# Moving half of the probability scaling to GpSimd and half of the transposed copies to VectorE in a sparse-attention decoder kernel

## The chip, the cores and the metric

The kernel runs on one core of a Trainium2 chip. The metric is the device time in microseconds (us) of one execution, as the median of several runs. The engines are called PE (TensorE), PEld (its weight loads), DVE (VectorE), ACT (ScalarE), POOL (GpSimd) and SP (SyncE, which issues DMAs).

## What is computed

The reference is a two-layer decoder trunk on 256 tokens of width 1024, in float32. Layer 0 mixes tokens with a gated MLP, layer 1 with a sparse attention of three branches (compressed, selected blocks, window); each layer ends in a squared-ReLU MLP of width 4096. With 256 tokens the selected-block branch selects all blocks and the window covers all tokens, so both are causal softmax attention, with two different K/V sets. There are 16 query heads in 4 groups of 4 heads, head size 64. What the change touches is this part:

```python
s_sel = jnp.einsum('bqghd,bgqmd->bghqm', qb, ks)
p_sel = masked_softmax(s_sel, kpos <= tq[None, None, None, :, None])
o_sel = jnp.einsum('bghqm,bgqmd->bqghd', p_sel.astype(vs.dtype), vs)
...
p_w = masked_softmax(s_w, mask_w)
o_win = jnp.einsum('bghqk,bkgd->bqghd', p_w.astype(vw.dtype), vw)
o = gb[..., 0:1] * ocb + gb[..., 1:2] * o_sel + gb[..., 2:3] * o_win
```

## The kernel before

The tokens are two chunks of 128 (ck 0 and 1). Each chunk is a Python generator that goes through gMLP, MLP, attention and MLP; `drive` (L968) takes steps of the two in turn, so that one chunk's matmuls lie beside the other's vector work. A scheduler then orders each engine's instructions once, when the program is built, by priority and by durations that it models; on the chip every engine runs its list in that order, and a waiting instruction holds up all behind it. Weights are split into a high and a low part as they arrive, by one ACT copy (L350) and one DVE subtraction (L351) of 128x1024 each, and every product is three matmuls (L375 to L377). SP issues the weight loads; POOL does memsets, the small reciprocal roots (L402, L411, L412, L619) and a few DMA issues.

In the attention, `queries` (L778) makes the transposed queries of two head groups, a pair p2. `scores` (L820) makes one group's scores of both branches on PE (L835, L837), their negated maxima on DVE (L838) and the exponentials on ACT with their sums (L842), in tiles `p` of 128 x 2 branches x 128 (ck 0) or 256 keys (ck 1). `weighted` (L848) is called once per chunk and pair, four times in all, with both groups of the pair (gg 0 and 1):

- Factors `cf` (L856, L857, DVE): gate over sum, one tiny tile per group.
- Scaling (L863, DVE): each head's row of probabilities times its factor, in place, SBUF to SBUF. Per branch four heads of gg 0, then four of gg 1: 16 instructions in a call, 64 in all.
- Per branch and block kc of 128 keys (one block for ck 0, two for ck 1): for each group four transposes on PE (L871) into one PSUM tile `ptp` of 128x512 (the pool has two buffers), and a copy `pT` to SBUF on ACT (L873); 24 copies in all.
- Products with the values (L876), gg 0 in columns 0 to 63 of the array and gg 1 in 64 to 127. The line `together(m, pTs[1][1])` (L879) makes the first group's product wait for the second group's copy, so that they run side by side.

`attend_cmp` (L881) then adds the compressed branch: a chain of small DVE operations `sm`, `cden`, `pc` (L892 to L906), two transposes (L909), an ACT copy (L912) and products (L915). The chunk's output projection y_mix follows in `nsa_out` (L948).

Of the kernel before, what the change touches and what calls it, by code (L numbers as in the profile page):

```python
# [10 lines left out]
AF = mybir.ActivationFunctionType  # L11
ALU = mybir.AluOpType
# [38 lines left out]
def trunk(ctx: ExitStack, tc: tile.TileContext, x, vec, rowv, first_w, ada_w, ada_b, norm_g, a_w_in, a_w_s, a_w_out,  # L51
          kv_w, cmp_w1, cmp_b1, cmp_w2, cmp_b2, b_w_in, gate_w, b_w_out, ff_w_in, ff_w_out, out):
    nc = tc.nc
# [16 lines left out]
    def pt_tile(name, dt=F32):  # L70
        return psT.tile([P, 512], dt, tag="t", name=name)
# [63 lines left out]
    def together(ins, last):  # L135
        tc.add_manual_dep(ins.ins, last.ins.name,
                          mybir.DependencyInfo(mybir.DependencyClass.Sync, mybir.DependencyReason.DATA),
                          reason="column tiles side by side")
# [253 lines left out]
    def small(name, n=1):  # L392
        return sp.tile([P, 16], F32, tag="small", name=name)[:, :n]
# [454 lines left out]
    def weighted(ck, p2, made, oT):  # L848

        V = at["V"]  # L850
        gate = at["gate"][ck]
        cfs = []
        for gg, (pr, den) in enumerate(made):
            g = 2 * p2 + gg
            cf = small(f"cf_{ck}_{g}", 8)
            nc.vector.reciprocal(cf, den)  # L856
            nc.vector.tensor_tensor(cf.rearrange("p (h r) -> p h r", r=2), cf.rearrange("p (h r) -> p h r", r=2),  # L857
                                    gate[:, 4 * g:4 * g + 4, 1:3], ALU.mult)
            cfs.append(cf)
        for br in range(2):  # L860
            for (pr, den), cf in zip(made, cfs):
                for h in range(4):
                    nc.vector.tensor_scalar(pr[h][:, br, :], pr[h][:, br, :], cf[:, h * 2 + br:h * 2 + br + 1],  # L863
                                            None, ALU.mult)
            for kc in range(ck + 1):
                pTs = []
                for gg, (pr, den) in enumerate(made):
                    g = 2 * p2 + gg
                    pt = pt_tile(f"ptp_{ck}_{g}_{br}_{kc}")
                    for h in range(4):  # L870
                        nc.tensor.transpose(pt[:, h * P:(h + 1) * P], pr[h][:, br, kc * P:(kc + 1) * P], ident)  # L871
                    pT = rp.tile([P, 512], F32, tag="rh", name=f"pT_{ck}_{g}_{br}_{kc}", bufs=4)
                    pTs.append((pT, nc.scalar.activation(pT, pt, AF.Copy)))  # L873
                for gg in range(2):
                    g = 2 * p2 + gg
                    m = nc.tensor.matmul(oT[64 * gg:64 * gg + 64, :], V[:, kc, br, g * 64:g * 64 + 64], pTs[gg][0],  # L876
                                         start=(br == 0 and kc == 0), stop=False)
                    if gg == 0:
                        together(m, pTs[1][1])  # L879
# [38 lines left out]
    def nsa(ck, parts):  # L918
        nm = f"mix1_{ck}"
        xT = tmp(f"xT_{nm}")  # L920
        for hf in range(2):
            nc.scalar.activation(xT[:, half(hf)], parts[hf], AF.Copy)
        kvpair = modulated(f"kv_{ck}", parts, "kvsh", "kvsc")
        yield from keys_values(ck, kvpair)
        pool = state["np"]
        bpair = modulated(f"b_{ck}", [xT[:, half(0)], xT[:, half(1)]], "sh11", "sc11")
        yield from gates(ck, bpair)
        hh = hl = None
        for p2 in range(2):
            yield from queries(ck, bpair, p2, pool)  # L930
            oT = y_tile(f"oT_{ck}_{p2}")
            made = []
            for gg in range(2):
                made.append((yield from scores(ck, 2 * p2 + gg, pool)))
            weighted(ck, p2, made, oT)
            if ck == 0:
                yield lambda: "cmp" in at
            attend_cmp(ck, p2, oT)
            if p2 == 0:
                o0 = oT  # L940
            else:
                hh, hl = hpair(f"o_{ck}")
                for i, o in enumerate((o0, oT)):
                    split_out(hh[:, 4 * i:4 * i + 4, :], hl[:, 4 * i:4 * i + 4, :], blocks(o))
            yield
        at[f"o{ck}"] = (hh, hl)
# [166 lines left out]
```

## Time and profile before

| | |
|---|---|
| median of 3 runs | 712.33 us (711.68 to 713.01) |
| the profiled execution, its own time | 708.8 us |
| its span in the profile | 707.1 us |
| busy: PE, DVE, ACT, POOL | 666.4, 475.2, 355.9, 37.0 us |
| instructions | 9173 |
| stage of the four `weighted` calls | 421.9 to 496 us |

A row of a group of instructions names its line, engine, operation, written tile <- read tiles, shapes and count; then busy time and mean duration in ns of one; then the idle time of the engine before them and what ended it. Busy time counts overlapping instructions once, so that count times mean can be more. A row of the timeline gives start and length in us of one instruction or of a run of like instructions, and in brackets idle time before it. A row of busy time by stretch gives the stretch, its length, the busy time (and instructions) of PE, PEld, DVE, ACT and POOL, the granted clock of TensorE as a share of 2.4 GHz, the share of the DMA engines, and GB/s.

### The profile page before, as it was taken

Reading aid. Unit: us, or ns where it says so; the run is one execution under the profiler, and the core shown is the slowest. Engines: PE = TensorE matmul, PEld = TensorE weight load, DVE = VectorE, ACT = ScalarE, POOL = GpSimd, SP = SyncE. Lnnn points to the kernel's source line nnn. Section 1 sums busy time; section 2 is a strip of 40 time slices with the busy share of each in tenths; the row PEclk is TensorE's granted clock in tenths of the full one; section 3 lists DMA queues with packets and bytes.
Section 4 is the critical chain, followed back from the end, with each engine's and each line's share of the span. In section 5 each row is a group of like instructions: output and inputs, shape, how many; then the busy total and the mean of one; then the engine's idle time right before and its main releaser. Section 6 shows DMA issues by size and latency. Waiting matters only on the chain.

```text
span 707.1 us, 9173 instructions
## 1 busy us (share of the span) xinstructions
PE 666.4 (94%) x3296; PEld 499.6 (71%) x3296; DVE 475.2 (67%) x712; ACT 355.9 (50%) x599; POOL 37.0 (5%) x70
## 2 busy tenths in 40 slices
PE   4899998999999999998899989989999999999996
PEld 1456765778888888876557666656778888888884
DVE  3546984998497886959875366665887545455524
ACT  3334345665535553454535476764656555455521
POOL 3001100100000000002000000000210000000000
PEclk9999999999999999999899999999999999999999
DMA  8887879779688979855675783200576656665101
GB/s 344 343 331 287 303 298 359 238 246 374 216 291 312 390 248 363 305 211 196 193 256 201 299 327 118 90 32 1 186 252 224 210 201 209 213 209 200 63 0 60
DMA packets 45535, 162.61 MB, mean 230 GB/s; under 512 B 5417, under 2 KB 5801, under 8 KB 45490
## 3 DMA queue, kind: packets, MB, share of 16 engines
q1 hardware_dynamic: 44928, 161.82, 64.1%
q8 instruction: 26, 0.43, 0.3%
q10 hardware_dynamic: 466, 0.20, 0.1%
q14 instruction: 19, 0.16, 0.1%
q0 software_dynamic: 96, 0.01, 0.0%
HBM read 160.96 MB, written 1.05 MB: 229 GB/s over the span
## 4 chain that ended last, share of the span: by engine, by line
PE 82%; DVE 5%; ACT 5%; DMA 3%; issue 2%; POOL 2%; SPq 0%; ACTq 0%; DVEq 0%; POOLq 0%
PE y_ff L377 8%; PE y_ff L375 8%; PE y_ff L376 8%; PE pa_fi L375 8%; PE pa_fi L377 8%; PE pa_fi L376 8%; PE pts_ff L488 2%; PE ptp L871 2%; PE pa_ain L376 2%; PE pa_ain L375 2%; PE oT L876 2%; PE pa_ain L377 2%; PE y_mix L375 2%; PE y_mix L376 2%; PE pa_kv L375 2%
## 5 line engine op out<-in xcount | busy, mean ns | idle before, releaser
L351 DVE TENSOR_TENSOR wl_fo<-w_fo,wh_fo 128x1024 fp32r<-128x1024 f32 x64 | 78.1, 1224 | 53.5 <-ACT wh_fo L350 53.3
L376 PE MATMUL y_ff<-wl_fo,rh_ff 128*128 128x512 f32 x256 | 103.0, 402 | 0.0
L375 PE MATMUL pa_fi<-wh_fi,hh_ff 128*128 128x512 f32 x256 | 100.3, 392 | 2.8 <-ACT hh_ff L380 2.8
L350 ACT ACTIVATE wh_fo<-w_fo 128x1024 fp32r<-128x1024 f32 x64 | 67.5, 1059 | 68.0 <-PE pa_fi L377 52.7
L375 PE MATMUL y_ff<-wh_fo,rh_ff 128*128 128x512 f32 x256 | 101.7, 397 | 0.0
L377 PE MATMUL y_ff<-wh_fo,rl_ff 128*128 128x512 f32 x256 | 101.3, 396 | 0.0
L376 PE MATMUL pa_fi<-wl_fi,hh_ff 128*128 128x512 f32 x256 | 99.9, 390 | 0.0
L377 PE MATMUL pa_fi<-wh_fi,hl_ff 128*128 128x512 f32 x256 | 99.6, 390 | 0.0
L351 DVE TENSOR_TENSOR wl_fi<-w_fi,wh_fi 128x1024 fp32r<-128x1024 f32 x64 | 77.5, 1224 | 28.4 <-ACT wh_fi L350 27.9
L350 ACT ACTIVATE wh_fi<-w_fi 128x1024 fp32r<-128x1024 f32 x64 | 67.1, 1058 | 52.2 <-PE y_ff L377 49.4
L375 PEld LDWEIGHTS pa_fi<-wh_fi,hh_ff 128*128 128x128 f32 x256 | 48.1, 188 | 13.5 <-ACT hh_ff L380 3.7
L375 PEld LDWEIGHTS y_ff<-wh_fo,rh_ff 128*128 128x128 f32 x256 | 48.2, 188 | 10.8
L377 PEld LDWEIGHTS y_ff<-wh_fo,rl_ff 128*128 128x128 f32 x256 | 48.3, 189 | 10.2
L376 PEld LDWEIGHTS y_ff<-wl_fo,rh_ff 128*128 128x128 f32 x256 | 48.4, 189 | 9.9
L377 PEld LDWEIGHTS pa_fi<-wh_fi,hl_ff 128*128 128x128 f32 x256 | 48.1, 188 | 10.1
L376 PEld LDWEIGHTS pa_fi<-wl_fi,hh_ff 128*128 128x128 f32 x256 | 48.1, 188 | 9.9
L502 ACT ACTIVATE r_ff<-pa_fi 128x512 f32<-128x512 f32 x32 | 19.1, 595 | 36.1 <-PE pa_fi L377 36.1
L195 DVE SCALAR_TENSOR_TENSOR acc_g<-aw_g,cact,acc_g 128x1024 f32<-128x1024 f32 x24 | 30.8, 1283 | 6.7 <-DMA aw_g<-in_ada_w_dram 4.1
L842 ACT ACTIVATE p<-sc,mx 128x128 f32<-128x128 f32 (+1 forms) x64 | 26.1, 428 | 11.2 <-DVE mx L838 11.2
L375 PE MATMUL pa_ain<-wh_ain,hh_mix 128*128 128x512 f32 x64 | 26.3, 422 | 2.5 <-ACT hh_mix L380 2.1
L838 DVE TENSOR_REDUCE mx<-sc 128x2 f32<-128x512 f32 (+1 forms) x24 | 16.0, 687 | 18.8 <-PE sc L837 18.8
L381 DVE TENSOR_TENSOR rl_ff<-pts_ff,rh_ff 128x512 fp32r<-128x512 f32 x32 | 21.9, 686 | 7.8 <-ACT rh_ff L380 7.7
(291 smaller groups left out, 1169.4 us busy)
## 6 DMA issues: line engine op xcount, KB each, us to landing
w_fi<-in_ff_w_in_dram SPq DMA_DIRECT2D x64, 512.0 KB, 4.6
w_fo<-in_ff_w_out_dram SPq DMA_DIRECT2D x64, 512.0 KB, 4.5
aw_g<-in_ada_w_dram SPq DMA_DIRECT2D x32, 512.0 KB, 4.2
aw_sh<-in_ada_w_dram SPq DMA_DIRECT2D x24, 512.0 KB, 5.0
aw_sc<-in_ada_w_dram SPq DMA_DIRECT2D x24, 512.0 KB, 5.8
aw_first<-in_first_w_dram SPq DMA_DIRECT2D x16, 512.0 KB, 6.8
w_ain<-in_a_w_in_dram SPq DMA_DIRECT2D x16, 512.0 KB, 6.7
w_kv<-in_kv_w_dram SPq DMA_DIRECT2D x12, 512.0 KB, 4.3
```

Source lines behind the costliest of these rows:

```text
L195: nc.vector.scalar_tensor_tensor(acc, raw, cs, acc, ALU.mult, ALU.add)
L350: i1 = nc.scalar.activation(hi[:, :n], raw[:, :n], AF.Copy)
L351: i2 = nc.vector.tensor_tensor(lo[:, :n], raw[:, :n], hi[:, :n].bitcast(F32), ALU.subtract)
L375: nc.tensor.matmul(ps, hh, wh, start=start, stop=False)
L376: nc.tensor.matmul(ps, hh, wl, start=False, stop=False)
L377: nc.tensor.matmul(ps, hl, wh, start=False, stop=stop)
L381: nc.vector.tensor_tensor(lo, src, hi.bitcast(F32), ALU.subtract))
L488: nc.tensor.transpose(pt[:, j * P:(j + 1) * P], src[:, j * P:(j + 1) * P], ident)
L502: nc.scalar.activation(r, pa, AF.Relu)
L838: nc.vector.tensor_reduce(mx.rearrange("p (i r) -> p i r", r=2), sc, AX.X, ALU.max, negate=True)
L842: nc.scalar.activation(pr[h0 + i][:, br, :], sc[:, i, br, :], AF.Exp, bias=mx[:, 2 * i + br:2 * i + br + 1], accum_out=den[:, n:n + 1])
L871: nc.tensor.transpose(pt[:, h * P:(h + 1) * P], pr[h][:, br, kc * P:(kc + 1) * P], ident)
```

## The change

The second group of each pair (gg 1) is scaled by POOL instead of DVE, and its transposed probabilities are copied by DVE instead of ACT. The first group stays: scaling on DVE, copies on ACT.

```diff
         for br in range(2):
             for (pr, den), cf in zip(made, cfs):
                 for h in range(4):
-                    nc.vector.tensor_scalar(pr[h][:, br, :], pr[h][:, br, :], cf[:, h * 2 + br:h * 2 + br + 1],
-                                            None, ALU.mult)
+                    eng = nc.vector if cf is cfs[0] else nc.gpsimd
+                    eng.tensor_scalar(pr[h][:, br, :], pr[h][:, br, :], cf[:, h * 2 + br:h * 2 + br + 1],
+                                      None, ALU.mult)
             for kc in range(ck + 1):
                 pTs = []
                 for gg, (pr, den) in enumerate(made):
...
-                    pTs.append((pT, nc.scalar.activation(pT, pt, AF.Copy)))
+                    pTs.append((pT, nc.vector.tensor_copy(pT, pt) if gg else nc.scalar.activation(pT, pt, AF.Copy)))
```

## Rows read from the trace of the kernel before

**Rows 1.** The page's first and fourth parts: engine totals and the chain that ended last.

```profile
PE 82%; DVE 5%; ACT 5%; DMA 3%; issue 2%; POOL 2%; SPq 0%; ACTq 0%; DVEq 0%; POOLq 0%
```

**Rows 2.** Busy time by stretch: PE, PEld, DVE, ACT, POOL, clock, DMA, GB/s.

```profile
420.00:425.00 5.00, 3.33 (x16) 2.63 (x15) 4.77 (x23) 4.60 (x19) 0.00 (x0) 0.76 0.98 376
...
445.00:450.00 5.00, 4.98 (x31) 3.35 (x30) 5.00 (x17) 4.02 (x12) 0.00 (x0) 1.00 0.02 3
...
460.00:465.00 5.00, 2.96 (x18) 2.29 (x18) 3.44 (x6) 3.83 (x16) 0.00 (x0) 1.00 0.31 107
465.00:470.00 5.00, 4.22 (x21) 3.56 (x22) 4.66 (x25) 4.24 (x18) 0.00 (x0) 0.70 0.00 0
...
485.00:490.00 5.00, 5.00 (x31) 3.22 (x30) 4.37 (x18) 2.24 (x5) 0.00 (x0) 1.00 0.00 0
```

**Rows 3.** Waits of PEld, 420 to 500 us: us in total, times, longest.

```profile
PEld ptp L871 <- DVE p L863: 3.2, 5, 1.8
PEld oT L876 <- ACT pT L873: 3.0, 8, 0.5
```

**Rows 4.** Groups by line and form: the moved operations and their nearest likes.

```profile
L863 DVE TENSOR_SCALAR p<-p,cf 128x256 f32<-128x256 f32 x32 | 8.7, 349 | 0.0
L863 DVE TENSOR_SCALAR p<-p,cf 128x128 f32<-128x128 f32 x32 | 6.6, 281 | 0.0
...
L690 DVE COPY kd<-pa_kv 128x512 f32<-128x512 f32 x2 | 1.4, 686 | 0.0
...
L873 ACT ACTIVATE pT<-ptp 128x512 f32<-128x512 f32 x24 | 13.8, 598 | 9.8 <-PE ptp L871 9.6
```

**Rows 5.** Groups by line and form on POOL, whole span.

```profile
L107 POOL CAST selr<-sel 128x256 fp32r<-128x256 f32 x1 | 0.4, 397 | 0.0
...
L96 POOL CAST onesr<-onef 128x128 fp32r<-128x128 f32 x1 | 0.3, 286 | 0.0
...
L412 POOL TENSOR_TENSOR rs_yff<-rs_yff,mhalf 128x1 f32<-128x1 f32 x4 | 2.3, 564 | 0.3
```

**Rows 6.** Timeline of POOL and DVE, at 4 us and at 60 us.

```profile
3.76 1.41 DVE L128 COPY cact<-cact 128x256 f32<-128x256 f32 x1
...
4.06 0.96 POOL L532 MEMSET lnrow<- 128x1024 f32 x1
...
60.67 1.39 POOL L619 TENSOR_TENSOR rs_ln<-rs_ln,mhalf 128x1 f32<-128x1 f32 x1
...
60.42 1.22 DVE L351 TENSOR_TENSOR wl_ain<-w_ain,wh_ain 128x1024 fp32r<-128x1024 f32 x1
```

**Rows 7.** Timeline of the second call (chunk 1, pair 0), 444 to 454 us.

```profile
444.51 0.16 DVE L857 TENSOR_TENSOR cf<-cf,gate 128x8 f32<-128x8 f32 x1
...
444.59 4.28 DVE L863 TENSOR_SCALAR p<-p,cf 128x256 f32<-128x256 f32 x16
...
446.87 2.01 ACT L873 ACTIVATE pT<-ptp 128x512 f32<-128x512 f32 x3
...
448.20 0.20 PEld L876 LDWEIGHTS oT<-pT,V 128*64 128x64 f32 x4 [0.26 <-ACT pT L873]
...
450.32 1.22 DVE L351 TENSOR_TENSOR wl_bout<-w_bout,wh_bout 128x1024 fp32r<-128x1024 f32 x1
...
451.66 0.68 DVE L838 TENSOR_REDUCE mx<-sc 128x4 f32<-128x512 f32 x1
```

**Rows 8.** Timeline of the fourth call (chunk 1, pair 1), 485 to 490 us.

```profile
484.99 0.16 DVE L857 TENSOR_TENSOR cf<-cf,gate 128x8 f32<-128x8 f32 x1
...
485.06 3.24 DVE L863 TENSOR_SCALAR p<-p,cf 128x256 f32<-128x256 f32 x12
...
487.03 1.09 ACT L873 ACTIVATE pT<-ptp 128x512 f32<-128x512 f32 x2 [0.65 <-PE ptp L871]
...
487.68 0.20 PEld L876 LDWEIGHTS oT<-pT,V 128*64 128x64 f32 x4 [0.39 <-ACT pT L873]
```

**Rows 9.** Timeline of the first and third calls (chunk 0): factors, scaling, second group's copy.

```profile
422.01 0.16 DVE L857 TENSOR_TENSOR cf<-cf,gate 128x8 f32<-128x8 f32 x1
...
422.09 3.02 DVE L863 TENSOR_SCALAR p<-p,cf 128x128 f32<-128x128 f32 x15
...
425.22 0.60 ACT L873 ACTIVATE pT<-ptp 128x512 f32<-128x512 f32 x1 [0.19 <-PE ptp L871]
...
466.63 0.16 DVE L857 TENSOR_TENSOR cf<-cf,gate 128x8 f32<-128x8 f32 x1
...
469.32 0.60 ACT L873 ACTIVATE pT<-ptp 128x512 f32<-128x512 f32 x1 [0.68 <-PE ptp L871]
```

## The prediction, made before the run

> **What bounds the kernel now.** I read first the engine totals and the chain that ended last: PE is busy for 666.4 of 707.1 us and makes up 82% of the chain [rows 1]. So time is won or lost where PE stands still or runs slowly, and nearly nowhere else. The change touches the 74 us of the four calls of `weighted`, so I read busy time by stretch there. PE is full in the two calls of chunk 1 (445 to 450 and 485 to 490 us), but not in those of chunk 0: it is busy 3.33 of 5 us from 420, and 2.96 and 4.22 of 5 us from 460 and 465, and the granted clock falls to a mean of 0.76 and 0.70 there, so part of it at 1.2 GHz [rows 2]. Then the waits of PE's weight loads: 3.2 us for a scaled probability and 3.0 us for a copy `pT` [rows 3]. These 6.2 us are what the change bears on directly. Last comes the timeline of each call, to see which instruction is last in each wait.
>
> In chunk 1's calls the second group's copy is what the products wait for: at 448.20 and 487.68 the loads of `oT` start as a run of ACT copies reaches gg 1 [rows 7, 8]. The line that holds both products until gg 1's copy is done makes that so in every iteration. The change moves exactly this copy, and the scaling ahead of it, to other engines.
>
> **What is moved.** 32 of the 64 scalings go to POOL. On DVE they come at a pitch of 4.28 / 16 = 0.27 us for 128x256 and 3.02 / 15 = 0.20 us for 128x128 [rows 7, 9], though one alone lasts 0.35 and 0.28 us [rows 4]. POOL has no multiplication by a column in this trace; its nearest rows are the casts of the same shapes, 0.40 and 0.29 us [rows 5]. I take these: one input, one output, the same number of elements. As a lower bound I take DVE's pitch, 0.27 and 0.20; as an upper one 1.39 us, which POOL needed for one column [rows 6]. That row tells more than a price, though: the same operation takes 0.56 us elsewhere [rows 5], and here it began while DVE subtracted a weight (60.42 to 61.64) and ended 0.42 us after it. The other direction shows too: a DVE copy of 128x256 took 1.41 us with a POOL memset of 0.96 us inside it [rows 6], where a scaling of that size takes 0.35 us [rows 4]. So I count that POOL and DVE keep each other out, an instruction at a time.
>
> The Trainium skill, "SBUF — State Buffer", section "SBUF: two separate sides", states this as a rule: DVE's second port pair is GpSimd's only one, it is held for a whole instruction, and a `tensor_scalar` from SBUF to SBUF on DVE can use it. No row here shows two scalings against each other. By the rule the sum below is +2.3 us; without it, some +1.2 us.
>
> If they take turns, gg 1's four scalings of a branch need four turns of both: 4 x (0.27 + 0.40) = 2.7 us for chunk 1 and 4 x (0.20 + 0.29) = 2.0 us for chunk 0, from the moment that gg 1's factor is there.
>
> - First call: the factor is there at 422.17 and the fourth scaling ends at 424.1; gg 1's copy started at 425.22 [rows 9], behind PE's transposes at the low clock. Hidden: 0.
> - Third call: 466.79 plus 2.0 is 468.8; the copy started at 469.32 [rows 9]. Hidden: 0. Were POOL let in only after DVE's eight, it would be 468.1 + 1.2 = 469.3, some 0.2 us late.
> - Second call: 444.67 plus 2.7 is 447.3, against 444.59 + 8 x 0.27 = 446.7 before. The last transposes take until about 447.7 and the copy on DVE 0.69 us, so the products start at 448.5, not at 448.20: +0.3 us. With POOL let in only after DVE's eight: +1.2 us. With no exclusion the scaling ends at 446.3, before today's: -0.3 us.
> - Fourth call: 485.15 plus 2.7 is 487.8, against 485.06 + 4 x 0.27 = 486.1 before. The products start at about 488.8 instead of 487.68: +1.1 us, of which I take 0.4 as covered by y_mix matmuls of the other chunk that lie between on PE: +0.7 us. If that cover is elsewhere in PE's list: +1.1. With no exclusion: +0.2.
>
> The second branch's scalings on POOL end 2 to 3 us ahead of their transposes in chunk 1 and cost nothing, unless three weight subtractions of 1.22 us get in turn before them.
>
> 12 of the 24 copies go to DVE. ACT needs 0.60 us for one; DVE's copy of the same shape out of PSUM takes 0.69 us [rows 4]. The eight waits for `pT` [rows 3] are for gg 1's copy, so each grows by 0.09: +0.7 us. The bound from below is zero, if PE has filler there. The gg 0 copy that goes on beside it on ACT was already off the path, since it is wanted one iteration later; so two copies at once gain nothing, except at 446.87, where three copies stand in a run on ACT [rows 7]; that gain is in the second call's +0.3.
>
> **The queues.** A DVE copy now waits for PE's transposes, which wait for POOL. Behind it on DVE stand the weight subtractions, the maxima `mx` of the other chunk and the compressed branch's chain; for `mx` ACT's exponentials wait. In front of it can stand a subtraction of 1.22 us, as at 450.32 [rows 7]. DVE is full at 445 to 450 us [rows 2]; for two of the three later copies of the second call I take a mean wait of half of it less what PE fills, 0.3 each: +0.6 us. Bounds: 0, and three whole subtractions, 3.7 us. On POOL's queue the scalings stand among memsets of `pc` and nothing that is wanted soon; the roots and the DMA issue come after the stage. SP's queue is not touched. What ACT is rid of (12 x 0.60 = 7.2 us) frees no wait that I found, since its copies mostly waited for PE (9.6 us [rows 4]). DVE gives 16 x 0.27 + 16 x 0.20 = 7.5 us and takes 12 x 0.69 = 8.3: even.
>
> **The sum.** 0.3 + 0.7 + 0.7 + 0.6 = +2.3 us. After the stage PE is the bound to the end, so it stays. Against the profiled execution (708.8 us, span 707.1 and 1.7 around it) that is 711.1. The median of the runs is 3.5 us above that execution, so I give the time against the median: 712.33 + 2.3 = 714.6 us. Both ends: with every bound on the slow side, 1.2 + 1.1 + 0.2 + 0.7 + 3.7 = +6.9 us, 719.2.
>
> **Rivals.**
>
> 1. *Faster: the chain ahead of the third call gets shorter.* In the second call DVE is done with its own scalings 8 x 0.27 = 2.1 us sooner, and the maximum `mx` of chunk 0, which ran at 451.66 behind them [rows 7], can come up to 2.1 us sooner, and with it exponentials and the third call. PE stands still for 2.8 us between 460 and 470 us [rows 2]; this closes up to 2.1 us of it: 710.2, at the utmost 709.5 if all 2.8 go. It decides if `mx` moves by more than the 1 us or so that the copies add. Against it: the list puts copies of gg 1 in front of `mx`, and much of that idle time is behind the query projection, which the change leaves alone. Chance 0.28.
> 2. *No difference: POOL and DVE do not hinder each other's scalings, or PE's filler covers it.* Then the terms are -0.3, +0.2, 0.7, 0.6: +1.2 us at most, down to 0: 712.3 to 713.5. For it: PE is full in both calls of chunk 1 [rows 2], so a late transpose can be met with other matmuls. Against it: the order of the list is fixed, and [rows 6]. Chance 0.24.
> 3. *Much slower: DVE's list stalls behind the copies.* If `mx` of the other chunk comes to stand behind two copies that wait for POOL, its exponentials and scores are late by 2 to 3 us in each call of chunk 1, and PE's clock falls in the gap, as it did from 465 us: +5 to +7 us, 717 to 719. Chance 0.12.
>
> That the change does not do what it says I exclude: the group's factor decides the engine, one to one.
>
> **The numbers.** The forecast, with mutual exclusion at the prices above, has 0.36. 0.2%, or 1.4 us, is about what a measurement of this kernel can tell from no change. Slower by more than that: 0.36 + 0.12 = 0.48; within it: 0.24; faster: 0.28. The range runs from 709.5, the utmost of the first rival, to 719.2, the sum of the slow bounds; the likeliest case alone spans 713.8 to 717.
>
> **What would show it.** POOL rows of 128x256 at L864 should last 0.4 us alone and 0.6 to 1.3 beside DVE work; DVE's eight scalings of a chunk 1 call should take more than 2.1 us. The wait of `oT` should be put down to DVE's copy, 0.1 us longer each, and the wait of `ptp` to POOL, longest in the fourth call. I am wrong if the sum of PE's idle time between 418 and 500 us does not rise, if `mx` of chunk 0 in the second call comes before 450.5, or if POOL's scalings take under 0.45 us while DVE scales.

## The result and the profile after

The changed kernel takes 722.46 us (median of 4 runs, 720.85 to 722.80) where the kernel before takes 712.67 us (4 runs, 711.68 to 714.52): a ratio of 1.0149, with a 95% interval of 1.0116 to 1.0182. That is 9.8 us slower. The sign was forecast; the size, +2.3 us, was not, and the time lies 3.3 us above the range. The profiled execution of the changed kernel has a span of 719.1 us in a time of 720.85 us.

The page's first part and the chain that ended last, for the changed kernel. They answer to [rows 1].

```profile
PE 674.7 (94%) x3296; PEld 502.9 (70%) x3296; DVE 477.4 (66%) x692; ACT 349.6 (49%) x587; POOL 63.3 (9%) x102
...
PE 79%; DVE 6%; POOL 4%; ACT 4%; DMA 3%; issue 3%; SPq 0%; ACTq 0%; POOLq 0%; DVEq 0%
```

POOL's share of the chain doubles, from 2% to 4%. PE has the same 3296 matmuls and yet is busy for 8.3 us more (674.7 against 666.4), and it stands still for 3.7 us more (719.1 - 674.7 = 44.4 against 707.1 - 666.4 = 40.7). So a part of the loss is waiting, and a part is PE working slowly.

Groups by line and form between 415 and 510 us, the moved operations on either engine. They answer to [rows 4].

```profile
L864 POOL TENSOR_SCALAR p<-p,cf 128x256 f32<-128x256 f32 x16 | 16.0, 1020 | 25.4 <-DVE cf L857 25.4
L864 POOL TENSOR_SCALAR p<-p,cf 128x128 f32<-128x128 f32 x16 | 10.7, 692 | 34.9 <-DVE cf L857 34.9
...
L864 DVE TENSOR_SCALAR p<-p,cf 128x256 f32<-128x256 f32 x16 | 6.0, 430 | 0.0
L864 DVE TENSOR_SCALAR p<-p,cf 128x128 f32<-128x128 f32 x16 | 3.5, 286 | 0.0
...
L874 DVE COPY pT<-ptp 128x512 f32<-128x512 f32 x12 | 8.3, 691 | 16.5 <-PE ptp L872 16.5
```

The first two rows carry the case: a scaling of 128x256 on POOL lasts 1.02 us on average and one of 128x128 lasts 0.69 us. The prediction had taken 0.40 and 0.29 us. DVE's copy came out at the price that was taken (0.69 us).

The waits of the same stretch. They answer to [rows 3].

```profile
ACT pT L874 <- PE ptp L872: 21.8, 11, 4.0
DVE pT L874 <- PE ptp L872: 16.5, 10, 2.6
...
PEld ptp L872 <- POOL p L864: 9.3, 16, 0.8
...
PEld oT L877 <- DVE pT L874: 0.7, 2, 0.4
```

There are 16 waits for POOL: four heads in each of the four calls, and by the timeline all of them are in the first of the two branches. The wait of the products for a copy, 3.0 us before, is 0.7 us: held up by POOL, PE now comes to the products late, and the copy is mostly there.

The second call (chunk 1, pair 0), timeline of all engines. It answers to [rows 7]; "x7" is a run of seven, so its time over seven is the pitch.

```profile
447.05 0.24 DVE L857 TENSOR_TENSOR cf<-cf,gate 128x8 f32<-128x8 f32 x2
...
447.40 2.87 DVE L864 TENSOR_SCALAR p<-p,cf 128x256 f32<-128x256 f32 x7
447.46 8.66 POOL L864 TENSOR_SCALAR p<-p,cf 128x256 f32<-128x256 f32 x8 [9.24 <-DVE cf L857]
...
448.77 0.44 PE L872 MATMUL ptp<-identr,p 128*128 128x128 f32 x2 [0.27 <-POOL p L864]
...
449.70 0.33 PE L872 MATMUL ptp<-identr,p 128*128 128x128 f32 x1 [0.49 <-POOL p L864]
...
450.63 0.44 PE L872 MATMUL ptp<-identr,p 128*128 128x128 f32 x2 [0.60 <-POOL p L864]
...
451.53 0.44 PE L872 MATMUL ptp<-identr,p 128*128 128x128 f32 x2 [0.46 <-POOL p L864]
...
451.89 0.69 DVE L874 COPY pT<-ptp 128x512 f32<-128x512 f32 x1 [1.62 <-PE ptp L872]
...
453.09 1.21 DVE L351 TENSOR_TENSOR wl_bout<-w_bout,wh_bout 128x1024 fp32r<-128x1024 f32 x1
453.14 0.20 PEld L877 LDWEIGHTS oT<-pT,V 128*64 128x64 f32 x4 [0.17 <-DVE p L864]
...
455.86 0.68 DVE L838 TENSOR_REDUCE mx<-sc 128x4 f32<-128x512 f32 x1
```

PE takes POOL's four heads one by one as they come, some 0.9 us apart, with little between. Both factors are there at 447.05 + 0.24 = 447.29; the products, the `oT` loads of L877, start 5.85 us later. Before it was 3.53 us (444.67 to 448.20, [rows 7]). So this call's gate opens 2.3 us later, where the prediction had +0.3. The fourth call has these two rows:

```profile
494.12 0.16 DVE L857 TENSOR_TENSOR cf<-cf,gate 128x8 f32<-128x8 f32 x1
...
501.04 0.30 PEld L877 LDWEIGHTS oT<-pT,V 128*64 128x64 f32 x4 [0.65 <-DVE cden L901]
```

There the span from the factor to the products goes from 2.53 us ([rows 8]) to 6.76 us (494.28 to 501.04; products of y_mix stand between), +4.2 us where it had +0.7. In the calls of chunk 0, where it had nothing, the copy of the second group starts 3.53 us after the factor (422.21 to 425.74) instead of 3.05, and 3.32 us (473.18 to 476.50) instead of 2.53 ([rows 9] for both): +0.5 and +0.8 us.

What this adds up to shows in the last products of each call, from the timeline of PE. First the kernel before:

```profile
436.03 1.09 PE L915 MATMUL oT<-pcT,vc 128*64 128x128 f32 x16
456.66 1.04 PE L915 MATMUL oT<-pcT,vc 128*64 128x128 f32 x16
475.58 1.09 PE L915 MATMUL oT<-pcT,vc 128*64 128x128 f32 x16
495.83 1.04 PE L915 MATMUL oT<-pcT,vc 128*64 128x128 f32 x16
```

Then the changed one:

```profile
438.37 1.09 PE L916 MATMUL oT<-pcT,vc 128*64 128x128 f32 x16
463.91 1.04 PE L916 MATMUL oT<-pcT,vc 128*64 128x128 f32 x16
484.67 1.09 PE L916 MATMUL oT<-pcT,vc 128*64 128x128 f32 x16
509.81 1.04 PE L916 MATMUL oT<-pcT,vc 128*64 128x128 f32 x16
```

The delay is 2.3 us after the first call, then 7.3, 9.1 and 14.0. Chunk 1's calls lose 4.9 us each, chunk 0's 2.3 and 1.8. The gate is 4.2 us of the fourth call's 4.9 but only 2.3 of the second's. Behind the second call's gate PE is full (10.75 of the 10.77 us up to the last products) and does 60 matmuls where it did 46 before, so part of that delay is work done in another order and not time lost. The stage behind gives 2 us back: the spans differ by 12.0.

The stretches in which PE works slowly, busy time by 5 us as in [rows 2].

```profile
420.00:425.00 5.00, 2.74 (x12) 1.45 (x11) 3.38 (x16) 3.78 (x18) 2.62 (x4) 0.82 0.99 388
425.00:430.00 5.00, 4.89 (x15) 2.44 (x15) 3.35 (x5) 2.80 (x5) 3.23 (x5) 0.50 0.07 26
...
445.00:450.00 5.00, 4.24 (x21) 3.33 (x19) 4.13 (x16) 2.46 (x9) 2.54 (x3) 0.79 0.00 0
450.00:455.00 5.00, 3.94 (x23) 2.44 (x22) 2.88 (x6) 1.28 (x3) 5.00 (x5) 1.00 0.02 3
...
470.00:475.00 5.00, 2.99 (x17) 1.90 (x16) 4.31 (x17) 4.24 (x20) 1.65 (x3) 0.94 0.24 88
475.00:480.00 5.00, 4.89 (x14) 2.17 (x15) 2.77 (x7) 0.91 (x2) 3.25 (x6) 0.50 0.00 0
```

In both calls of chunk 0 a stretch with 2.74 or 2.99 us of PE work in 5 is followed by one that runs wholly at the lower level, 1.2 GHz. PE looks full there (4.89 of 5), but between 425 and 430 us it does 15 matmuls where it did 26 before. The first call's first four products with the values show the price of it, before and then after:

```profile
426.71 1.08 PE L876 MATMUL oT<-pT,V 128*64 128x512 f32 x4
...
427.55 1.98 PE L877 MATMUL oT<-pT,V 128*64 128x512 f32 x4
```

Twice (1 - clock) times the length, summed over the stretches from 410 to 520 us, is the time at 1.2 GHz: some 20.5 us, against 6.8 us in the profile of before. At half speed 13.7 us more are at most 6.9 us of lost work, which can be most of the 8.3.

The profile of before stands at one end in this, though: its granted clock is 0.990, while 71 other timed executions of that kernel list 0.971 to 0.989, with a median of 0.985. By the same formula over the whole span these have a median of 21.3 us at 1.2 GHz, the four of the changed kernel 33.2 us. Over the 71, a microsecond more at 1.2 GHz goes with 0.30 us more of span (correlation 0.80); at half speed all through it would be 0.50. So 11.9 us more are some 3.6 to 6 us of the 9.8, and the rest is waiting. That split is worked out and not shown by a run.

### The profile page after: what moved, and what is told of

The parts are those of the page before. It is cut to its first block, busy times and chain, and to the rows that moved or that the text cites. A ratio compares the mean times of both kernels' runs of the same rounds, so it can differ in the third digit from the quotient of the medians.

```text
span 719.1 us, 9159 instructions
## 1 busy us (share of the span) xinstructions
PE 674.7 (94%) x3296; PEld 502.9 (70%) x3296; DVE 477.4 (66%) x692; ACT 349.6 (49%) x587; POOL 63.3 (9%) x102
## 4 chain that ended last, share of the span: by engine, by line
PE 79%; DVE 6%; POOL 4%; ACT 4%; DMA 3%; issue 3%; SPq 0%; ACTq 0%; POOLq 0%; DVEq 0%
PE y_ff L377 8%; PE y_ff L375 8%; PE y_ff L376 8%; PE pa_fi L375 7%; PE pa_fi L377 7%; PE pa_fi L376 7%; PE pts_ff L488 2%; PE oT L877 2%; POOL p L864 2%; PE pa_ain L375 2%; PE pa_ain L376 2%; PE ptp L872 2%; PE pa_ain L377 2%; PE pa_kv L375 2%; PE pa_kv L376 1%
## 5 line engine op out<-in xcount | busy, mean ns | idle before, releaser
L842 ACT ACTIVATE p<-sc,mx 128x128 f32<-128x128 f32 (+1 forms) x64 | 26.1, 427 | 15.1 <-DVE mx L838 15.1
L864 POOL TENSOR_SCALAR p<-p,cf 128x128 f32<-128x128 f32 (+1 forms) x32 | 26.8, 856 | 60.3 <-DVE cf L857 60.3
```

Of the source, the lines that this page charges most:

```text
L842: nc.scalar.activation(pr[h0 + i][:, br, :], sc[:, i, br, :], AF.Exp, bias=mx[:, 2 * i + br:2 * i + br + 1], accum_out=den[:, n:n + 1])
L864: eng.tensor_scalar(pr[h][:, br, :], pr[h][:, br, :], cf[:, h * 2 + br:h * 2 + br + 1], None, ALU.mult)
```

## The experiments

The theories have the letters that the expectations use. Theory P, formed on the rows above: POOL's multiplication costs over twice what was taken, the first branch's transposes of group 1 wait for it head by head, and PE's clock falls in the waits. Rivals: C, the copies on DVE (their price, and what queues behind them); L, POOL and DVE keeping each other out; S, the order of PE's list, in which the changed kernel has the two groups' transposes in turns in the first three calls, where before four mostly stood behind four. All ratios are to the kernel before, timed beside each experiment on the same chip; the three groups of runs had medians of 711.12, 712.07 and 710.90 us for it.

**The two parts alone.** The first (e1) keeps the scaling on POOL and puts all copies back on ACT; the second (e2) moves only the copies.

```
e1   pTs.append((pT, nc.scalar.activation(pT, pt, AF.Copy)))
e2   nc.vector.tensor_scalar(...)        # L863 as before
```

> Only the scaling of the second group moves to POOL; all 24 copies stay on ACT. Theory P (POOL's scaling is dear, some 0.6 us for 128x128 and 0.9 us for 128x256, and PE waits for it in its fixed order): nearly all of the loss stays, 719 to 723 us beside 712 to 713 of before, POOL's pitch again 0.6 to 1.1 us. Theory C (the copies on DVE are what costs): most of the loss goes, 712 to 716 us.

> Only the second group's copies move to DVE; all 64 scalings stay on DVE. Theory P: within 2 us of before, 711 to 715 us; the term of the prediction for this part was +0.7 for the copies and +0.6 for the queue. Theory C: 718 us or more, with long waits of the products for DVE's copy.

Measured: the scaling alone 724.42 us, 1.0203 [1.0156, 1.0251]; the copies alone 712.20 us, 1.0017 [0.9990, 1.0044]. The first is 1.4 us above its range, the second inside. The loss is there without the copies on DVE and not with them alone, so C falls. The copies on DVE cost +1.2 us at the median, with an interval that holds no cost as well as 3 us. Beside the scaling the ratio is 1.0203 without them and 1.0149 with them; the intervals overlap, so that they help there is not shown.

**The second branch alone.** POOL scales only the second branch of group 1; copies on ACT, and in a later run on DVE.

```
-eng = nc.vector if cf is cfs[0] else nc.gpsimd
+eng = nc.gpsimd if cf is cfs[1] and br == 1 else nc.vector
```

> POOL scales the second group in the second branch only (16 scalings, which have 2 to 3 us before their transposes); the first branch and all copies stay as before. Theory P: four scalings of 0.6 or 0.9 us are 2.4 to 3.7 us, about as long as that slack, so 712 to 716 us. Theory L (POOL and DVE keep each other out, so that any POOL work beside DVE's scaling costs): half of the loss stays, 716 to 719 us, and DVE's own scalings are longer than 0.35 us.

> As the changed kernel, but POOL scales the second group in the second branch only; the copies of the second group stay on DVE. Theory P: the second branch's scalings have time until their transposes, so 708 to 714 us, near the run with ACT's copies (0.9993 of before). If POOL work beside DVE work costs by itself: 716 us or more.

Measured: 711.29 us, 0.9993 [0.9964, 1.0021], 0.7 us below its range, and with the copies on DVE 710.17 us, 0.9994 [0.9971, 1.0017], inside. POOL's scalings are as dear as in the changed kernel (1.03 and, in the later run, 1.00 us for 128x256) and PE has no wait for POOL among its waits. So the price hurts in the first branch, right behind the factor, and is hidden in the second.

**A cheaper operation on POOL.** In place of group 1's scaling POOL copies the probabilities onto themselves; group 1 stays unscaled.

```
-eng.tensor_scalar(pr[h][:, br, :], pr[h][:, br, :], cf[...], None, ALU.mult)
+nc.gpsimd.tensor_copy(pr[h][:, br, :], pr[h][:, br, :])     # group 1 only
```

> As the changed kernel, but POOL copies the second group's probabilities in place instead of multiplying them, so that this group's scaling is left out. Theory P: a copy costs what the casts cost, 0.29 and 0.40 us; at that price the sum of the prediction should hold, 713 to 717 us. Theory L, and theory S (the order of PE's list, with the two groups' transposes in turns, is what costs): the loss stays, 719 us or more.

Measured: 706.04 us, 0.9943 [0.9915, 0.9971]. This is below the range and below the kernel before, but it is no test of the price alone: the copies no longer read the factor and ran behind the exponentials. In POOL's timeline the first call's first four start at 414.12 us, released by `ACT p L842`, 8.0 us ahead of the call's first factor (422.14). The experiment had taken away two things, a price and a wait, so the next ones put the wait back.

**The price alone.** Two kernels (e5 and e6) whose lists on PE, DVE and ACT are those of the changed kernel; on POOL the copy, or a multiplication by the constant 0.5, waits for the factor. Group 1 is unscaled in the first and halved in the second.

```
+made_cf = nc.vector.tensor_tensor(cf..., gate..., ALU.mult)
 ...
e5   i = nc.gpsimd.tensor_copy(pr[h][:, br, :], pr[h][:, br, :])
e6   i = nc.gpsimd.tensor_scalar(pr[h][:, br, :], pr[h][:, br, :], 0.5, None, ALU.mult)
+    together(i, made_cf)
```

> The lists of PE, DVE and ACT are those of the changed kernel, instruction for instruction; POOL copies the second group's probabilities in place instead of multiplying them (the scaling of this group is left out), and each copy still waits for the group's factor. So only the price of POOL's instruction differs. Theory P (price): POOL's pitch is 0.26 and 0.36 us, as of the casts, and the time is 704 to 712 us. Theory S (the order of the lists) and theory L (mutual exclusion of POOL and DVE): 718 us or more.

> As the run before, but POOL multiplies by a constant (the second group's factor is left out) instead of copying. If the column operand makes POOL's scaling dear, the pitch is that of the copy, 0.26 and 0.36 us, and the time is that of the run before. If the arithmetic itself is dear, the pitch stays at 0.6 and 0.9 us and the time at 720 to 724 us.

Measured: with the copy 712.82 us, 1.0003 [0.9972, 1.0033]; with the constant 719.53 us, 1.0089 [1.0058, 1.0120]. The first is 0.8 us above its range, the second 0.5 us below the range for dear arithmetic. Group rows, one wait and DVE's scalings in the second call, of the kernel with the copy:

```profile
L867 POOL COPY p<-p 128x256 f32<-128x256 f32 x16 | 6.3, 443 | 25.5 <-DVE cf L857 25.5
L867 POOL COPY p<-p 128x128 f32<-128x128 f32 x16 | 4.1, 307 | 35.6 <-DVE cf L857 35.6
...
PEld ptp L875 <- POOL p L867: 1.4, 7, 0.3
...
445.48 2.77 DVE L864 TENSOR_SCALAR p<-p,cf 128x256 f32<-128x256 f32 x7
```

The same of the kernel with the constant:

```profile
L867 POOL TENSOR_SCALAR p<-p 128x256 f32<-128x256 f32 x16 | 14.5, 935 | 24.5 <-DVE cf L857 24.5
L867 POOL TENSOR_SCALAR p<-p 128x128 f32<-128x128 f32 x16 | 9.3, 612 | 39.7 <-DVE cf L857 39.7
...
PEld ptp L875 <- POOL p L867: 7.6, 16, 0.7
```

The only difference between the two is what POOL does to a tile, and it is worth 719.53 - 712.82 = 6.7 us. Worked out: four first-branch operations are 4 x 0.49 = 2.0 us dearer in a call of chunk 1 and 4 x 0.31 = 1.2 us in one of chunk 0 by these means, 6.4 us in four calls. The agreement is no proof, since this sum leaves out the clock and what other work hides. At 0.44 and 0.31 us, nearly the prices that the prediction took, no loss shows. This pair settles the case for P, and it speaks against C and S too, since copies and order were those of the changed kernel. It speaks against L as far as DVE is the one held up: beside POOL's copies DVE's pitch is 2.77 / 7 = 0.40 us, as slow as in the changed kernel (0.41), and yet no loss shows.

**The order of PE's list.** Group 1's transposes held behind group 0's.

```
+t_ = nc.tensor.transpose(...)
+if gg:
+    behind(t_, prev)
```

> The changed kernel with one more rule for the scheduler: on PE the second group's four transposes come behind the first group's four, as they mostly did in the kernel before, and not in turns with them. Theory S (the turns make PE wait for POOL early): the first group's copy and filler go ahead, 713 to 718 us. Theory P: PE waits as long a little later, 719 to 723 us.

Measured: 721.68 us, 1.0133 [1.0092, 1.0173], with 8.7 us of waits for POOL in place of 9.3. S falls: the interval holds the changed kernel's ratio. The fourth call says the same: there the changed kernel's list already has the first group's four transposes ahead (the last starts at 494.53 us, and the wait for POOL's first head ends at 495.57), and it loses 4.9 us as the second call does.

**Less on POOL.** Two of group 1's four heads (e7); the same with the copies on ACT (e12); one head of each group (e10).

```
e7, e12   eng = nc.gpsimd if cf is cfs[1] and h >= 2 else nc.vector     # e12: copies on ACT
e10       eng = nc.gpsimd if h == 3 else nc.vector
```

> As the changed kernel, but POOL scales only heads 2 and 3 of the second group; DVE scales the other six of each branch. Theory P: two scalings of 0.92 us are about as long as DVE's six of 0.27 us, so PE's wait nearly goes: 707 to 714 us. If any wait of PE for POOL brings the loss, whatever its length: 717 us or more.

> POOL scales heads 2 and 3 of the second group, DVE the other six, and all copies are on ACT as before. Theory P: 708 to 714 us. If the copies on DVE gave the gain of the run with two heads and DVE copies (0.9965 of before): 711 to 714 us; if POOL's two heads gave it: 707 to 711 us.

> POOL scales head 3 of both groups in both branches (16 scalings instead of 32, as many as in the run with two heads of the second group), DVE the other six; copies as in the changed kernel. Theory P: two scalings on POOL beside six on DVE, 707 to 714 us, as the run with two heads; but the first group's last head now also waits for POOL, so rather the upper half. If the run with two heads was faster by chance of the lists: 712 to 716 us.

Measured: two heads 710.30 us, 0.9965 [0.9936, 0.9993]; with the copies on ACT 715.34 us, 1.0062 [1.0035, 1.0088]; one head of each group 713.23 us, 1.0040 [1.0019, 1.0061]. The first is inside its range; the second is above all three of its ranges, a miss; the third lies in both of its ranges and so separates nothing. One wait and POOL's second call in the kernel with two heads and copies on DVE:

```profile
PEld ptp L872 <- POOL p L864: 1.2, 3, 0.8
...
445.40 4.06 POOL L864 TENSOR_SCALAR p<-p,cf 128x256 f32<-128x256 f32 x4 [5.97 <-DVE cf L857]
```

POOL's two first-branch heads now take 2 us beside DVE's six at some 0.4 us, and 3 waits of the 16 are left. Of the versions that leave nothing of the computation out it is the one whose interval lies below the kernel before: by 0.35% at the ratio, in one comparison with ten runs of it, and by 0.07% at the interval's end. Whether that holds elsewhere was not tried. With ACT's copies the waits for POOL are the same (1.3 us in 3), the wait of the products for a copy is back at 3.0 us in 8, and the time is above that of before. So fewer waits for POOL do not explain the gain by themselves: with one head of each group they are down to 0.4 us in 2, and that kernel is slower than before too. Why the one of the three is faster and the two others are slower stays open.

**Keeping PE busy in the waits.** Ten idle matmuls in front of each of group 1's four transposes in the first branch's first block, 160 in all, into the same tile that the transposes then overwrite.

```
+if gg and br == 0 and kc == 0:
+  for _ in range(10):
+      d_ = nc.tensor.matmul(pt[:, h * P:(h + 1) * P], identr, at["kT"][:, 0, 0, 0, 0:P], start=True, stop=True)
+      behind(d_, t_)
```

> The changed kernel with ten idle matmuls of 128 columns ahead of each of the second group's transposes in the first branch's first block (160 in all, their results are overwritten by the transposes), so that PE works while it waits for POOL; the groups' transposes come one group after the other. If the fall of PE's clock makes a good part of the loss: the granted clock of the stage stays near 1.00 in the calls where it fell, and the time is 713 to 719 us in spite of some 10 us of added matmuls. If the loss is idle time alone: 722 to 730 us.

Measured: 740.57 us, 1.0419 [1.0380, 1.0457]. This is a miss, above both ranges. The matmuls had been counted at some 10 us; their group has 28.1 us, 28.1 / 160 = 0.18 us each, a part of them at the lower level. Busy time by 5 us of that kernel, in a call of chunk 0 and one of chunk 1:

```profile
420.00:425.00 5.00, 2.71 (x15) 2.21 (x16) 4.77 (x19) 4.74 (x21) 1.45 (x2) 0.91 0.98 351
425.00:430.00 5.00, 5.00 (x26) 5.00 (x26) 4.50 (x8) 4.23 (x6) 5.00 (x5) 0.50 0.48 180
...
450.00:455.00 5.00, 4.98 (x35) 4.06 (x34) 3.70 (x16) 3.52 (x13) 1.46 (x2) 1.00 0.02 3
455.00:460.00 5.00, 5.00 (x47) 4.99 (x47) 4.90 (x11) 1.64 (x6) 5.00 (x5) 1.00 0.10 24
```

In the second call the clock stays at 1.00 with PE full, where the changed kernel's had gone to 0.79 between 445 and 450 us; in the first it had fallen before the idle matmuls came, in a gap ahead of the call, and stayed low through full stretches. So the matmuls cost more than the clock gave back, and the size of the clock's part stays without a run.

## Why the prediction came out as it did

**The step that failed** is the price of POOL's scaling: "its nearest rows are the casts of the same shapes, 0.40 and 0.29 us [rows 5]. I take these: one input, one output, the same number of elements." The casts did tell the price of POOL's copy (0.44 and 0.31 us on average); they did not tell that of a multiplication. With the copy in its place the time is that of before, within an interval of -0.28% to +0.33%. That holds the forecast's +0.3% as well as no change, so the runs do not speak against the sum at the prices in it. The price was wrong by a factor of 2.1 to 2.3 at the pitch (0.61 and 0.92 us) and of 2.4 to 2.6 by the mean of one (0.69 and 1.02 us).

**The range failed by the same step.** The text named an upper bound for the operation, 1.39 us, and then added up "every bound on the slow side" with 0.40 us inside each of them. With 1.39 us carried through, four turns in a call of chunk 1 are 4 x (0.27 + 1.39) = 6.6 us instead of 2.7, and two such calls alone move the slow end from 719.2 to some 727 us. The measured 0.92 us lay between the named ends.

**Hidden in calls 1 and 3: wrong by the same price.** Four scalings at 0.61 us and more put the copy 0.5 and 0.8 us later there, and each of these calls loses about 2 us. PE's work behind the wait runs at 1.2 GHz (the rows from 425 and 475 us): the first four products of the first call take 1.98 us instead of 1.08.

**The clock was placed with the wrong case.** The forecast had no term for it. The third rival had it, "PE's clock falls in the gap", but as a consequence of DVE's list stalling behind two copies. The gap came from POOL. A part of the rival's stall is there: the maximum `mx` of the other chunk comes 8.6 us behind the second call's factor (447.29 to 455.86 us) where it came after 7.0 us (444.67 to 451.66, [rows 7]). But the loss does not need it. With the scaling on POOL and all copies on ACT `mx` comes after 7.0 us again (447.50 to 454.51), and the ratio is 1.0203. So Rival 3's size, +5 to +7 us, was nearer than the forecast by luck, with another mechanism.

**Turns of POOL and DVE: half right.** The forecast counted that they keep each other out, an instruction at a time. Two of POOL's runs in the second call, from the timeline cut to short windows, beside the DVE rows above:

```profile
447.46 1.26 POOL L864 TENSOR_SCALAR p<-p,cf 128x256 f32<-128x256 f32 x1 [9.24 <-DVE cf L857]
...
453.25 1.97 POOL L864 TENSOR_SCALAR p<-p,cf 128x256 f32<-128x256 f32 x1
```

While DVE scales, POOL's first scaling takes 1.26 us and the ones behind it come 0.93 us apart. In the fourth call, once DVE's scalings are over, they come 0.90 us apart (496.42, 497.32, 498.22 us), so DVE's scalings hardly hold POOL up. POOL holds DVE up: its pitch goes from 0.27 us [rows 7] to 2.87 / 7 = 0.41 us. The wait of a whole instruction is there with the weight subtraction: it ends at 453.09 + 1.21 = 454.30 us, and the POOL scaling that began inside it ends 0.92 us later, at 455.22, as if it had begun at the subtraction's end. [rows 6] had shown much the same. Four scalings of the first branch took 4.0 us; without exclusion they would be 4 x 0.92 = 3.7, in strict turns 4 x (0.27 + 0.92) = 4.8. The error in this step is a few tenths per call.

The Trainium skill, "SBUF — State Buffer", section "SBUF: two separate sides", states that GpSimd and a DVE operation with two SBUF inputs, or in a mode that takes both ports, shut each other out for a whole instruction. The trace agrees for the subtraction, which has two inputs, with the 0.92 us behind its end; for the scalings, which have one, it shows only DVE's slowing from 0.27 to 0.41 us, and not the turns that the prediction counted.

**Right, by the runs:** the gate is group 1's transposes, then its copy, then both products (the 16 waits); the copies on DVE are about neutral (+1.3 us forecast for them and their queue, +1.2 us measured, in an interval that also holds no cost); the second branch has slack (two runs at 0.999); the wait for `ptp` is put down to POOL and is longest in the fourth call (0.85 us). **Wrong beside the price:** the wait of the products for a copy, forecast to grow by 0.7 us, fell to 0.7 us in all, since PE came to it later than the copy. Of the three signs that were to refute the forecast none appeared: PE's idle time between 418 and 500 us rose (from 6.9 to 11.4 us), `mx` came later, and no POOL scaling took under 0.45 us. They tested the direction and not the size. The one sign for the size, "0.4 us alone", failed at once. The "0.6 to 1.3 beside DVE work" came true (1.26 and 0.93 us), but by luck: it was meant as 0.4 us and a wait for DVE, and the operation itself takes that long.

## What to carry to other kernels

A price taken from another operation on the same engine is a guess as long as only shape and operand count agree; name its bounds, and then carry both bounds through every term in which it stands, the range included. Work moved off a busy engine is paid where someone waits for its first piece: ask how long the slower engine needs for the first tiles behind the event that releases them, and give it those that have slack (the second branch here; with a group's last heads only one of three versions gained). Where the engine that bounds the kernel comes to wait several times in a row, look at its granted clock behind the waits as well as at the waits.

## What the runs showed of the hardware

- POOL's in-place operations on 128 partitions of f32, by the pitch of eight in the fourth and third calls: the copy 2.99 / 8 = 0.37 us for 256 elements and 2.07 / 8 = 0.26 us for 128; the multiplication by a constant 6.59 / 8 = 0.82 and 4.09 / 8 = 0.51 us; by a column 7.39 / 8 = 0.92 and 4.90 / 8 = 0.61 us. The first ones of each eight run beside DVE's scalings. So 128 elements more cost 0.9 ns each in the copy and 2.4 ns each in the multiplication, and a column in place of a constant costs 0.10 us at either size.

The rows for 256 elements are from the timeline of POOL in the fourth call. The kernel with the copy:

```profile
489.26 2.99 POOL L867 COPY p<-p 128x256 f32<-128x256 f32 x8 [17.24 <-DVE cf L857]
```

The kernel with the constant:

```profile
496.54 6.59 POOL L867 TENSOR_SCALAR p<-p 128x256 f32<-128x256 f32 x8 [16.28 <-DVE cf L857]
```

The changed kernel:

```profile
494.45 7.39 POOL L864 TENSOR_SCALAR p<-p,cf 128x256 f32<-128x256 f32 x8 [16.19 <-DVE cf L857]
```

The Trainium skill, "GPSIMD Engine Reference", section "Engine selection", says that one-input elementwise work on GpSimd is roughly at line rate; if DVE's pitch of 0.27 us for 256 elements [rows 7] is taken as that rate, the copy with 0.37 us comes near it, and the multiplication by a constant, which has one input too, does not with 0.82 us.

- A stretch in which PE is half idle can be paid twice: in the changed kernel the 5 us behind stretches of 2.74 and of 2.99 us of PE work were granted 0.50, the lower level, though PE was busy for 4.89 us of them.
- Executions of one kernel differ in this by themselves: the 71 of the kernel before list granted clocks from 0.971 to 0.989, and their spans go with it (correlation 0.80).
